# Encoder layer: two small constants widened, adaLN dots, token-block loads and one row of sums moved

## The chip, the cores and the metric

The kernel runs on one core of one Trainium2 chip. The metric is the device time of one execution in microseconds (us). The core has a matrix engine (TensorE, PE in the profile, with its weight loads as PEld), a vector engine (VectorE, DVE), a scalar engine (ScalarE, ACT), GpSimd (POOL) and SyncE (SP), which issues most of the loads from its queue. All tiles live in on-chip memory of 128 partitions; a tile's address is its offset within each partition.

## The reference

One residual layer of a bidirectional encoder, for one sequence of 1024 tokens and 1024 channels. What matters:

```python
mod = silu(c) @ w_ada + b_ada                       # 6 x 1024, shifts, scales, gates
h = rmsnorm(x, norm1_g) * (1 + sc1) + sh1
u, v, q, k, va, gate_a, gate_b = split(h @ w_in)
a_out = gelu(u) * (W_s rmsnorm(gelu(v)) + b) @ w_a  # per chunk of 128 positions
b_out = window_attention(q, k, va) @ w_b            # |t - s| <= 128, ALiBi, sinks
merged = sigmoid(gate_a) * a_out + sigmoid(gate_b) * b_out
x = x + gt1 * (merged @ w_o)
h2 = rmsnorm(x, norm2_g) * (1 + sc2) + sh2
x = x + gt2 * ((silu(h2 @ w_gate) * (h2 @ w_up)) @ w_out)
```

All values are fp32.

## The kernel before

Every product is made of three fp32r matmuls: each operand is split into a high part (a cast on ACT, tiles named ...h) and a low part (a subtraction on DVE, ...l), and high x high, high x low and low x high are added up in PSUM. A weight arrives as a `raw` tile of 128 x 1024, is split into `wh` and `wl` (`unit`), and serves 12 to 24 matmuls of 512 columns. `raw`, `wh` and `wl` have three buffers each.

The stages, in order:

- `half(0)` and `half(1)` work through 512 tokens each: norm and adaLN, the q, k, v and u projections, attention and the gating branch, then the loop over `d` (line 1117 on) with the branch products `w_a`, `w_b`: 24 matmuls per d. The unit of d + 1 is split in iteration d. Beside it run jobs. In half 0 these prepare half 1's tokens (`x_mod`), and adaLN dots run. In half 1 they are `block_sums`: the gates of d = 2 to 7 are computed for both halves of tokens and channels at once from sums of blocks, seven products in place of eight, and the jobs make those sums.
- `block_sums(k, part, ...)` needs four tiles of 128 x 512: a0 and a1 (half 0's tokens, `x0d`, in the two buffers of `hs`), b0 and b1 (half 1's, `x1sd`, in the two of `xs`). `block_load(k)` fetches all four; `block_part` makes the high part at once and gives back the step that makes the low part. Part 0 of chunk k runs in iteration 2k, part 1 in 2k + 1.
- the gates for d = 2 to 7 (loop in line 1185).
- the output projection `w_o` of half 0 and then of half 1 (loop in line 1261), a unit and 24 matmuls per d. The operand `m0` of half 0 is in `mid` tiles, `m1` of half 1 in `j` tiles. Each iteration adds the squares of its rows to `ss` (`sumsq`). Half 0's row of root mean squares is made in half 1's loop: `col_rstd` (four small matmuls with `ss`, in two passes each, then a power on POOL) after the matmuls of d = 0, `spread` after those of d = 1, and from then on `mod2(d - 1)` makes the second adaLN input of half 0.
- the FFN's products for both halves, again by seven block products per block of weights (operands `h`, `j` and `mid`), and the output product.

adaLN: each of the 48 columns of `mod` is a dot of silu(c) with a row of weights, on DVE (1.22 us for 128 x 1024). Sixteen are made at the start. The other 32 come in the order of `ada_queue`, each from one `raw` tile: `ada_load` fetches the next, `ada_next` makes a dot and fetches the next one (unless told not to), `ada_half` does one in two halves of 512 with tiles of `hs` and a small tile `part`. They lie in half 0's branch loop (one per d for d = 0 to 6 and a second at d = 2: eight), in half 1's projections (five), in the gates' loop (five and five halves), and in half 0's output projection (one per d and a second at d = 4: nine).

Order: `load` keeps the loads on SP's queue in program order, so a load that waits for its buffer holds those behind it. Instructions of an engine keep the written order where `in_order` is set (the first projection, the attention's part of the code and d < 2 of the branch loop, the last two d of the output projection); elsewhere the order is laid out when the program is built.

Addresses: the pools follow each other: `const` (ends with `shd`), `wpool` (raw, wh, wl), `hpool` (h), `mid`, `t2` (t2, hs, xs), `small` (ss, part and others), `cpool` (silu_c), then either the attention's tiles or the tiles `j`, and in the last stage raw2, oh and ol. Every tile takes a multiple of 32 bytes. `raw`, `wh` and `wl` are 4096 bytes a buffer, `h`, `mid` and `j` 8192. In the program of before `wpool` begins at 32 past a multiple of 64, and with it all the large tiles.

Of the kernel before, what the change touches and what calls it, by code (L numbers as in the profile page):

```python
# [8 lines left out]
F32 = mybir.dt.float32  # L9
# [3 lines left out]
ALU = mybir.AluOpType  # L13
# [3 lines left out]
P = 128  # L17
# [21 lines left out]
def kernel(  # L39
# [47 lines left out]
    const = ctx.enter_context(pool("const"))  # L87
# [25 lines left out]
    def stream(tag):  # L113
        return t2.tile([P, 512], F32, tag=tag, name=nm(tag), bufs=2)
# [18 lines left out]
    def sm(n, name):  # L133
        return small.tile([P, n], F32, tag=name, name=nm(name))

    def load(dst, src):
        tc.keep_in_program_order(nc.sync.dma_start(dst, src))
# [395 lines left out]
    def ada_half(more=True):  # L533
        if not ada_halves:
            return
        col, gain, t = ada_halves.pop(0)
        part = sm(1, "part")
        for i, acc_col in enumerate((acc_mod[:, col : col + 1], part)):
            V.scalar_tensor_tensor(out=t[i], in0=t[i], scalar=1.0,
                                   in1=silu_c[:, i * 512 : (i + 1) * 512], op0=ALU.mult,  # L540
                                   op1=ALU.mult, accum_out=acc_col)
        added(acc_mod[:, col : col + 1], part)
        ada_end(col, gain)
        if more:
            ada_half_load()
# [7 lines left out]
    def added(dst, src):  # L553
        V.tensor_tensor(dst, dst, src, op=ALU.add)
# [14 lines left out]
        V.tensor_tensor(s, m[:, :, 0], m[:, :, 1], op=ALU.add)  # L569
        rstd(s, NT, rcol[1])  # L570

    shd = const.tile([P, 8], F32, tag="shd", name="shd")
    dsh, nsh = shd[:, :4], shd[:, 4:]
    blk = {}

    def block_load(k):
        chunk = [stream(x) for x in ("hs", "hs", "xs", "xs")]
        for i, src in enumerate((x0d, x1sd)):
            for q in range(2):
                load(chunk[2 * i + q], src[4 * q + k])  # L580
        return chunk

    def block_part(name, k, src, kind, bias=None):
        if k == 0:
# [6 lines left out]
        return lambda: V.scalar_tensor_tensor(out=l, in0=src, scalar=bias, in1=h.bitcast(F32),  # L591
                                              op0=ALU.add, op1=ALU.subtract)

    def block_sums(k, part, chunk, kinds):
        a0, a1, b0, b1 = chunk
        c = slice(k, k + 1)
        if part == 0:
            if k == 0:
                V.tensor_tensor(dsh, mod[:, SH1 + 4 : SH1 + 8], mod[:, SH1 : SH1 + 4], op=ALU.subtract)
                V.tensor_scalar(nsh, mod[:, SH1 + 4 : SH1 + 8], -1.0, None, op0=ALU.mult)  # L600
            low = block_part("B21", k, a1, kinds[0], mod[:, SH1 + 4 + k : SH1 + 5 + k])
            V.tensor_tensor(b1, b1, b0, op=ALU.subtract)
            low()
            low = block_part("T3", k, b1, kinds[1], dsh[:, c])
            V.tensor_tensor(a1, a0, a1, op=ALU.subtract)
            V.tensor_tensor(b0, a0, b0, op=ALU.subtract)
            low()
            return
        low = block_part("B11", k, a0, kinds[0], mod[:, SH1 + k : SH1 + k + 1])
        added(a1, b1)  # L610
        low1 = block_part("T1", k, b0, kinds[1])
        low()
        low = block_part("T4", k, a1, kinds[2])
        low1()
        V.scalar_tensor_tensor(out=a0, in0=b1, scalar=-1.0, in1=a0, op0=ALU.mult, op1=ALU.subtract)
        low()
        block_part("N2", k, a0, kinds[1], nsh[:, c])()

    raws, gunits, acc = {}, {}, {}

# [69 lines left out]
    def half(hf):  # L690
# [62 lines left out]
        for k in range(KT):  # L753
            if hf == 0:
                x = xt[k]
# [340 lines left out]
        if hf == 0:  # L1096
            ada_load()
            x_spread()
            x_load(0)
            x_load(1)  # L1100
            jobs.extend((k, lambda k=k: x_mod(k)) for k in range(KT))
            jobs.append((7, lambda: x_mod(KT)))
        else:
            apool_ctx.close()
            jpools.append(ffn_ctx.enter_context(pool("j", 6, reuse_waits="tile")))
            kinds = (lambda: midt(F32R, 4)), (lambda: jt(F32R, 4)), hid
            blk["B22"] = (hH[1], hL[1])
            chunk = [block_load(0)]

            def block_job(k, part):  # L1110
                block_sums(k, part, chunk[0], kinds)
                if part and k < 3:
                    chunk[0] = block_load(k + 1)

            jobs.extend((2 * k + p, lambda k=k, p=p: block_job(k, p)) for k in range(4) for p in range(2))

        for d in range(KT):
            in_order[0] = d < 2
            if 0 < d < KT - 1:
                wab.append(unit(None, V, abr.pop(0)))  # L1120
                if d + 2 + hf < KT:
                    abr.append(raw_unit(w_ab[d + 2 + hf]))
            elif d:
                if hf == 0:
                    early.append(unit(None, V, early_raw[0]))
                else:
                    gate_prep_b(2)
            if hf and d == 5:
                gate_load(2)
            if hf and d == 6:  # L1130
                gate_prep_a(2)
            ms = []
            for br, t in ((1, (oH, oL)), (0, (gH, gL))):
                pb = mm_bank()
                for k in range(4):
                    kc = slice(br * Q + k * P, br * Q + (k + 1) * P)
                    mm3(pb, (wab[d][0][:, kc], wab[d][1][:, kc]), (t[0][:, k, :], t[1][:, k, :]),
                        k == 0, k == 3)
                if d < 2:
                    sg = gates.pop(0)  # L1140
                    V.scalar_tensor_tensor(out=sg, in0=sg, scalar=1.0, in1=pb, op0=ALU.add,
                                           op1=ALU.mult)
                    ms.append(sg)
                else:
                    c = tmp()
                    A.copy(c, pb)
                    j = 2 * hf + br
                    store(pd[d][:, j * Q : (j + 1) * Q], c)
            if d < 2:
                V.tensor_tensor(ms[0], ms[0], ms[1], op=ALU.add)  # L1150
                store(md[hf][d], ms[0])
            in_order[0] = False
            while jobs and jobs[0][0] <= d:
                jobs.pop(0)[1]()
            if hf == 0:
                if d == 2:
                    ada_next()
                ada_next(d < 6)
                if d > 5:
                    early_raw.append(raw_unit((w_q[0], w_kv[0])[d - 6]))  # L1160

# [84 lines left out]
    for hf in range(2):  # L1246
# [14 lines left out]
        for d in range(KT):  # L1261
            wo = wo_next
            if d < KT - 1:
                wo_next = unit(w_o[d + 1])
            elif hf == 0:
                wo_next = unit(w_o[0])
            else:
                raw1 = raw_unit(w_gate[1])
                raw2.append(raw_unit(w_gate[2]))
            if hf == 1 and d == 6:  # L1270
                early.append(unit(w_gate[0], V))
            in_order[0] = hf == 1 and d > 5
            if hf == 1 and d in (2, 4):
                early.append(first_unit(d // 2 - 1))
            xk = stream("xs")
            load(xk, x_rows(hf, d))
            pw = mm_bank()
            for k in range(KT):
                kc = slice(k * P, (k + 1) * P)
                mm3(pw, (wo[0][:, kc], wo[1][:, kc]),  # L1280
                    (m[k // 4][0][:, k % 4, :], m[k // 4][1][:, k % 4, :]), k == 0, k == KT - 1)
            if hf == 1:
                if d == 0:
                    col_rstd(sums[0], NT, rcol[2])
                elif d == 1:
                    rb = spread(rcol[2], NT)
                if d:
                    mod2(d - 1)
            x1 = tmp() if hf == 0 else x1B[d // 4][:, d % 4, :]
            V.scalar_tensor_tensor(out=x1, in0=pw, scalar=mod[:, GT1 + d : GT1 + d + 1], in1=xk,  # L1290
                                   op0=ALU.mult, op1=ALU.add)
            sumsq(x1, d == 0, ss)
            store(x1d[d * P : (d + 1) * P, hf * HALF : (hf + 1) * HALF], x1)
            if hf == 0:
                if d == 0:
                    m1 = m_tiles(jt)
                else:
                    m_split(m1, d - 1)
                m_load(m1, 1, d)
                if d == KT - 1:  # L1300
                    m_split(m1, d)
                ada_next()
                if d == 4:
                    ada_next()
            if hf == 1 and d == KT - 1:
                mod2(d)
                early.append(unit(None, V, raw1))
# [195 lines left out]
    def low(src, t, k):  # L1503
        V.tensor_tensor(t[1][:, k, :], src, t[0][:, k, :].bitcast(F32), op=ALU.subtract)
# [360 lines left out]
```

## Time and profile before

| what | us |
|---|---|
| median of 3 runs (1273.71 to 1276.75) | 1275.17 |
| the profiled execution | 1270.48 |
| its span, first to last instruction | 1268.7 |
| PE busy in the span | 1234.8 |
| DVE busy | 911.9 |
| ACT busy | 572.5 |
| POOL busy | 161.1 |

The mean granted clock of TensorE is 0.994. A row of the profile reads: engine, operation, out<-in by the program's names with shapes, count, then busy time and mean ns of one, then the engine's idle time before it with what ended it. In a timeline the first number is the start in us from the span's start, the second the duration of the (merged) row. Nearly all instructions have one line, 76, since a helper there records them; tiles tell them apart. Matmuls overlap: one lasts about 390 ns, and the next begins before it has ended, so the time that a matmul takes is read from one start to the next.

### The profile page before, as it was taken

What the parts mean: (1) busy time and instruction counts of PE and PEld (TensorE: products, weight loads), DVE (VectorE), ACT (ScalarE), POOL (GpSimd) and SP (SyncE); (2) the same over time, 40 slices, a digit from 0 to 9 for tenths busy, and PEclk for the clock granted to TensorE, in tenths of its full rate; (3) what the DMA queues carried; (4) which work ended last, traced back from release to release, by engine and by line L of the source; (5) the groups of instructions that cost most, each with busy time, mean ns of one, the idle gap of its engine ahead of it and who ended that gap; (6) DMA issues with size and microseconds to landing.
All of it is one profiled execution on the core that took longest, in us unless ns stands there. A gap on an engine that the chain in (4) does not pass through costs nothing.

```text
span 1268.7 us, 15580 instructions
## 1 busy us (share of the span) xinstructions
PE 1234.8 (97%) x5634; PEld 1014.8 (80%) x5634; DVE 911.9 (72%) x1496; ACT 572.5 (45%) x930; POOL 161.1 (13%) x202
## 2 busy tenths in 40 slices
PE   6999998999999999999999999999999999999998
PEld 4888886888887787787888887888888887888887
DVE  9898885487888787976698756666666676455646
ACT  5567954267866333434444333333333334433341
POOL 1124332023321000001100000000110000010001
PEclk9999999999999999999999999999999999999999
DMA  9632179522247536697612353454654549896652
GB/s 369 240 100 96 38 245 320 166 85 66 59 146 244 215 138 228 216 331 233 242 57 100 135 197 136 162 199 182 215 167 176 188 166 332 287 325 189 195 164 100
DMA packets 76271, 236.28 MB, mean 186 GB/s; under 512 B 9121, under 2 KB 9121, under 8 KB 70178
## 3 DMA queue, kind: packets, MB, share of 16 engines
q1 hardware_dynamic: 60626, 163.45, 38.4%
q0 software_dynamic: 15568, 71.84, 15.3%
q8 instruction: 44, 0.72, 0.2%
q14 instruction: 33, 0.27, 0.1%
HBM read 178.11 MB, written 57.15 MB: 185 GB/s over the span
## 4 chain that ended last, share of the span: by engine, by line
PE 60%; issue 13%; DMA 11%; DVE 10%; ACT 5%; POOL 1%; SPq 0%; DVEq 0%; ACTq 0%; POOLq 0%
PE at L76 31%; PE mm L76 28%; DVE mid L76 3%; DVE wl L76 2%; DMA raw<-in_w_ada_dram 2%; DMA raw<-in_w_o_dram 2%; DMA raw<-in_w_ab_dram 2%; ACT wh L76 1%; ACT lb L76 1%; ACT mid L76 1%; DVE raw L76 1%; DMA mid<-in_w_ada_dram 1%; DVE xs L76 1%; DMA wo<-in_w_out_dram 1%; DMA hs<-md 1%
## 5 line engine op out<-in xcount | busy, mean ns | idle before, releaser
L76 ACT CAST wh<-raw 128x1024 fp32r<-128x1024 f32 x155 | 162.3, 1050 | 199.4 <-PE mm L76 52.7
L76 DVE TENSOR_TENSOR wl<-raw,wh 128x1024 fp32r<-128x1024 f32 x141 | 172.0, 1221 | 89.2 <-ACT wh L76 85.6
L76 PE MATMUL mm<-mid,wh 128*128 128x512 f32 x704 | 219.3, 393 | 2.6 <-ACT t L76 1.2
L76 PEld LDWEIGHTS mm<-mid,wh 128*128 128x128 f32 x704 | 132.4, 189 | 32.7 <-ACT t L76 1.6
L76 PE MATMUL at<-j,wh 128*128 128x512 f32 x464 | 145.5, 394 | 0.0
L76 PE MATMUL mm<-mid,wl 128*128 128x512 f32 x352 | 138.4, 393 | 3.2 <-DVE wl L76 3.2
L76 PE MATMUL mm<-wh,h 128*128 128x512 f32 x384 | 131.1, 404 | 2.9 <-ACT h L76 2.1
L76 PEld LDWEIGHTS at<-j,wh 128*128 128x128 f32 x464 | 87.1, 188 | 20.5
L76 DVE TENSOR_TENSOR wl<-ws,wh 128x1024 fp32r<-128x1024 f32 (+1 forms) x55 | 62.0, 1127 | 44.5 <-ACT wh L76 44.5
L76 PE MATMUL at<-j,wl 128*128 128x512 f32 x232 | 91.8, 395 | 0.5 <-DVE wl L76 0.5
L76 PE MATMUL mm<-j,wh 128*128 128x512 f32 x288 | 91.6, 399 | 0.0
L76 PE MATMUL at<-h,wh 128*128 128x512 f32 x288 | 89.1, 390 | 0.7 <-DVE mid L76 0.7
L76 PEld LDWEIGHTS mm<-wh,h 128*128 128x128 f32 x384 | 72.8, 192 | 17.9 <-ACT h L76 3.0
L76 PE MATMUL mm<-h,wh 128*128 128x512 f32 x272 | 84.6, 392 | 0.0
L76 PEld LDWEIGHTS mm<-mid,wl 128*128 128x128 f32 x352 | 66.5, 189 | 19.0 <-DVE wl L76 5.0
L76 ACT CAST wh<-ws 128x1024 fp32r<-128x1024 f32 (+1 forms) x55 | 53.5, 973 | 57.9 <-DVE ws L76 41.3
L76 PE MATMUL mm<-wl,h 128*128 128x512 f32 x192 | 76.4, 398 | 0.0
L76 PEld LDWEIGHTS mm<-j,wh 128*128 128x128 f32 x288 | 54.7, 190 | 12.6
L76 PEld LDWEIGHTS at<-h,wh 128*128 128x128 f32 x288 | 53.8, 188 | 12.2 <-DVE mid L76 1.1
L76 DVE TENSOR_TENSOR ol<-raw,oh 128x1024 fp32r<-128x1024 f32 x30 | 36.7, 1224 | 32.4 <-ACT oh L76 32.1
L76 PEld LDWEIGHTS mm<-h,wh 128*128 128x128 f32 x272 | 50.6, 188 | 10.5
L76 ACT ACTIVATE xs<-xs 128x512 f32<-128x512 f32 x21 | 13.3, 633 | 99.2 <-DVE xs L76 99.2
(273 smaller groups left out, 2544.9 us busy)
## 6 DMA issues: line engine op xcount, KB each, us to landing
raw<-in_w_gate_dram SPq DMA_DIRECT2D x28, 512.0 KB, 5.2
raw<-in_w_ada_dram SPq DMA_DIRECT2D x27, 512.0 KB, 5.5
tA<-hid POOLq DMA_DIRECT2D x11, 1024.0 KB, 5.2
tB<-hid POOLq DMA_DIRECT2D x11, 1024.0 KB, 5.1
wo<-in_w_out_dram POOLq DMA_DIRECT2D x22, 512.0 KB, 6.1
wS<-wo POOLq DMA_DIRECT2D x11, 1024.0 KB, 5.2
raw<-wS SPq DMA_DIRECT2D x44, 256.0 KB, 3.7
raw<-tB SPq DMA_DIRECT2D x44, 256.0 KB, 4.5
```

The costliest lines, as they stand in the source:

```text
L76: ins = f(*args, **kw)
```

## The change

Five edits. `shd` gets 16 columns, of which 8 are used, and `part` 16, of which 1 is used. `block_load` fetches one tile by name, and each of a chunk's four tiles is fetched as soon as its predecessor has been read for the last time; `block_sums` does B21, T3, B11 and T4 in part 0, and T1 and N2 in part 1. In half 0's branch loop the second dot of d = 2 and the dot of d = 6 are gone, and in half 0's output projection d = 3 and d = 5 have two dots as d = 4 does. Half 0's `col_rstd` stands after the matmuls of d = 1, its `spread` after those of d = 2, and `mod2` follows with 0 at d = 2, 1 and 2 at d = 3, then one per d.

```diff
@@ ada_half
-        part = sm(1, "part")
+        part = sm(16, "part")[:, :1]
@@ half 1's blocks
-    shd = const.tile([P, 8], F32, tag="shd", name="shd")
-    dsh, nsh = shd[:, :4], shd[:, 4:]
+    shd = const.tile([P, 16], F32, tag="shd", name="shd")
+    dsh, nsh = shd[:, :4], shd[:, 4:8]
     blk = {}
 
-    def block_load(k):
-        chunk = [stream(x) for x in ("hs", "hs", "xs", "xs")]
-        for i, src in enumerate((x0d, x1sd)):
-            for q in range(2):
-                load(chunk[2 * i + q], src[4 * q + k])
-        return chunk
+    chunk = {}
+
+    def block_load(k, name):
+        if k < 4:
+            chunk[name] = stream("hs" if name[0] == "a" else "xs")
+            load(chunk[name], (x0d if name[0] == "a" else x1sd)[4 * int(name[1]) + k])
...
-    def block_sums(k, part, chunk, kinds):
-        a0, a1, b0, b1 = chunk
+    def block_sums(k, part, kinds):
         c = slice(k, k + 1)
+        a0, a1, b0, b1 = (chunk[x] for x in ("a0", "a1", "b0", "b1"))
...
             V.tensor_tensor(b1, b1, b0, op=ALU.subtract)
             low()
             low = block_part("T3", k, b1, kinds[1], dsh[:, c])
+            low1 = block_part("B11", k, a0, kinds[0], mod[:, SH1 + k : SH1 + k + 1])
             V.tensor_tensor(a1, a0, a1, op=ALU.subtract)
-            V.tensor_tensor(b0, a0, b0, op=ALU.subtract)
+            added(a1, b1)
             low()
+            low = block_part("T4", k, a1, kinds[2])
+            low1()
+            low()
+            block_load(k + 1, "a1")
             return
-        low = block_part("B11", k, a0, kinds[0], mod[:, SH1 + k : SH1 + k + 1])
-        added(a1, b1)
+        V.tensor_tensor(b0, a0, b0, op=ALU.subtract)
         low1 = block_part("T1", k, b0, kinds[1])
+        V.scalar_tensor_tensor(out=a0, in0=b1, scalar=-1.0, in1=a0, op0=ALU.mult, op1=ALU.subtract)
+        low = block_part("N2", k, a0, kinds[1], nsh[:, c])
+        low1()
+        block_load(k + 1, "b0")
         low()
-        low = block_part("T4", k, a1, kinds[2])
-        low1()
-        V.scalar_tensor_tensor(out=a0, in0=b1, scalar=-1.0, in1=a0, op0=ALU.mult, op1=ALU.subtract)
-        low()
-        block_part("N2", k, a0, kinds[1], nsh[:, c])()
+        block_load(k + 1, "b1")
+        block_load(k + 1, "a0")
@@ half(1), before the loop over d
-            chunk = [block_load(0)]
-
-            def block_job(k, part):
-                block_sums(k, part, chunk[0], kinds)
-                if part and k < 3:
-                    chunk[0] = block_load(k + 1)
-
-            jobs.extend((2 * k + p, lambda k=k, p=p: block_job(k, p)) for k in range(4) for p in range(2))
+            for x in ("a1", "b0", "b1", "a0"):
+                block_load(0, x)
+            jobs.extend((2 * k + p, lambda k=k, p=p: block_sums(k, p, kinds))
+                        for k in range(4) for p in range(2))
@@ half(0), in the loop over d
             if hf == 0:
-                if d == 2:
-                    ada_next()
-                ada_next(d < 6)
+                ada_next(d < 5)
@@ the output projection
             if hf == 1:
-                if d == 0:
+                if d == 1:
                     col_rstd(sums[0], NT, rcol[2])
-                elif d == 1:
+                elif d == 2:
                     rb = spread(rcol[2], NT)
-                if d:
-                    mod2(d - 1)
+                for i in {2: (0,), 3: (1, 2), 4: (3,), 5: (4,), 6: (5,), 7: (6,)}.get(d, ()):
+                    mod2(i)
...
                 ada_next()
-                if d == 4:
+                if 2 < d < 6:
                     ada_next()
```

## The prediction

> **What bounds the kernel now.** I read the page first: the span and the engines' shares.
>
> ```profile
> span 1268.7 us, 15580 instructions
> PE 1234.8 (97%) x5634; PEld 1014.8 (80%) x5634; DVE 911.9 (72%) x1496; ACT 572.5 (45%) x930; POOL 161.1 (13%) x202
> ```
>
> TensorE (PE) is busy for 97% of the span, so there are only two ways to gain: the 33.9 us in which it is idle (1268.7 - 1234.8), and the time of one matmul. I therefore read the busy time by stages next: us of the stretch, then each engine's busy time and count, the granted clock, the DMA engines' share and GB/s.
>
> ```profile
> 214.00:226.00 12.00, 8.03 (x28) 6.21 (x27) 5.09 (x8) 1.69 (x3) 1.54 (x3) 0.73 0.70 239
> 342.00:409.00 67.00, 64.64 (x297) 53.52 (x295) 55.26 (x84) 43.89 (x71) 16.11 (x19) 0.97 0.58 190
> 527.00:576.00 49.00, 48.71 (x215) 39.87 (x214) 39.04 (x62) 18.31 (x25) 4.86 (x9) 1.00 0.91 321
> 576.00:586.00 10.00, 6.85 (x28) 5.29 (x27) 4.96 (x6) 4.09 (x5) 1.57 (x2) 0.83 0.94 311
> 632.00:1000.00 368.00, 367.64 (x1599) 299.37 (x1598) 259.16 (x363) 131.48 (x187) 24.55 (x46) 1.00 0.46 162
> 1060.00:1140.00 80.00, 80.00 (x354) 66.18 (x354) 41.23 (x38) 34.62 (x35) 4.41 (x7) 1.00 0.92 327
> 342.00:1268.00 926.00, 912.15 (x3987) 743.85 (x3985) 641.04 (x869) 364.48 (x484) 71.41 (x118) 1.00 0.57 195
> ```
>
> Apart from the start, PE is short of work at three places, and at each of them the clock falls below 1.00: the seam of the two halves (214 to 226), the branch products of half 1 (342 to 409), and the seam of the two output projections (576 to 586). From 632 on PE is full, and only the time of one matmul counts.
>
> **Part 1: adaLN dots.** At the seam of the halves the timeline (start, duration, engine, instruction, in brackets idle time and what ended it) shows this:
>
> ```profile
> 211.45 7.97 SPq L137 DMA_DIRECT2D raw<-in_w_ada_dram  x2
> 216.57 0.40 PE L76 MATMUL mm<-wl,h 128*128 128x512 f32 x1
> 217.83 1.22 DVE L76 SCALAR_TENSOR_TENSOR raw<-raw,silu_c 128x1024 f32<-128x1024 f32 x1 [6.41 <-DMA raw<-in_w_ada_dram]
> 218.99 1.22 DVE L76 TENSOR_TENSOR wl<-raw,wh 128x1024 fp32r<-128x1024 f32 x1
> 220.26 0.58 PE L76 MATMUL at<-wl,h 128*128 128x256 f32 x1 [3.29 <-DVE wl L76]
> 223.20 0.84 PE L76 MATMUL at<-wh,h 128*128 128x256 f32 x3
> 223.84 0.63 PE L76 MATMUL mm<-wh,h 128*128 128x512 f32 x1
> 224.27 0.63 PE L76 MATMUL mm<-wl,h 128*128 128x512 f32 x1
> ```
>
> DVE stands 6.41 us at the dot of d = 6, whose weights landed late. Behind it in DVE's queue is the low part of w_kv, and PE waits for that: from 216.57 + 0.23 to 220.26, 3.46 us. Afterwards PE runs at half clock: 223.84 to 224.27 is 0.43 for a matmul that takes 0.227 elsewhere (part 4). Some ten such matmuls until 226 lose 0.2 each, the seven 256 wide ones (223.20 to 223.84 for three, 0.21 each, against about 0.12) another 0.65: 2.6 us. The change takes the second dot of d = 2 and that of d = 6 out of this loop. DVE then has nothing before the low part of w_kv, which can run near 213. That is 3.46 + 2.6 = 6.1, and I take **-6.0**. Late next would be the second unit of w_q, which DVE can split a microsecond later. Bounds: -7.5 if the 0.7 us before 216.23 go too, -2 if another load of the three `raw` buffers is late in its place.
>
> The two dots go to the output projection of half 0, where d = 3, 4 and 5 now have two each. Two dots are 2 x (1.22 + 0.3) = 3 us of DVE, which has 49 - 39 = 10 us free there. Their weights are the dearer part:
>
> ```profile
> 528.20:558.20 30.00, 30.00 (x135) 24.82 (x133) 24.64 (x42) 11.11 (x16) 3.24 (x6) 1.00 0.97 336
> 554.67 1.23 DVE L76 SCALAR_TENSOR_TENSOR raw<-raw,silu_c 128x1024 f32<-128x1024 f32 x1
> 558.95 1.23 DVE L76 TENSOR_TENSOR wl<-raw,wh 128x1024 fp32r<-128x1024 f32 x1 [2.14 <-ACT wh L76]
> 560.23 0.50 PE L76 MATMUL mm<-mid,wl 128*128 128x512 f32 x1 [0.29 <-DVE wl L76]
> ```
>
> The DMA engines are 97% busy here, and 2 x 0.52 MB at 336 GB/s are 3.1 us more. Today's one double dot (554.67) already made the next w_o unit late: its low part waited 2.14 us and PE about 0.45. The SP queue hands out `w_o`, `x`, `md` and these loads in order, so each load of w_o stands behind two of w_ada. I take **+1.5** for three doubles in place of one; bounds 0 (prefetched in time) and +5 (all the added transfer time and more ends on PE).
>
> **Part 2: token blocks by need.** In half 1's branch products:
>
> ```profile
> 391.19 0.72 ACT L76 ACTIVATE mid<-hs,mod 128x512 fp32r<-128x512 f32 x1 [2.61 <-DMA hs<-x0d]
> 391.95 0.75 DVE L76 SCALAR_TENSOR_TENSOR mid<-hs,mod,mid 128x512 fp32r<-128x512 f32 x1 [3.06 <-ACT mid L76]
> 397.96 1.22 DVE L76 TENSOR_TENSOR wl<-raw,wh 128x1024 fp32r<-128x1024 f32 x1
> 398.07 2.12 SPq L137 DMA_DIRECT2D hs<-x0d  x2
> 399.23 0.50 PE L76 MATMUL mm<-mid,wl 128*128 128x512 f32 x1 [2.36 <-DVE wl L76]
> ```
>
> DVE loses 3.06 us to a block that SP could ask for only when the buffer freed last was free (all four loads are issued together, and they hold the queue for 2.12 us, with w_ab, w_ga and w_gb behind them). The low part at 397.96 comes that much later, and PE waits 2.36 for it; the clock of 0.97 over 67 us is another 1.5 or so at half speed. Loaded one by one, a1 is asked for some five operations of DVE earlier. Work is only moved: part 0 has seven operations on DVE instead of five, part 1 four instead of six, about 0.7 each. 3.06 us less on DVE cover the 2.36. But what part 0 gains in length (1.4 us) can again stand ahead of a low part of w_ab, so of the 4 us I take **-3**; bounds -4.5 and +2 (the longer part 0 makes two units late by 1 us).
>
> **Part 3: sum of squares of half 0, one block later.**
>
> ```profile
> 576.76 1.04 ACT L76 CAST wh<-raw 128x1024 fp32r<-128x1024 f32 x1 [3.66 <-DMA raw<-in_w_o_dram]
> 577.84 1.22 DVE L76 TENSOR_TENSOR wl<-raw,wh 128x1024 fp32r<-128x1024 f32 x1 [2.82 <-ACT wh L76]
> 579.72 1.05 PE L76 MATMUL at<-ones,ss 128*128 128x1 f32 x8 [3.15 <-DVE ss L76]
> 580.63 0.71 PE L76 MATMUL mm<-j,wh 128*128 128x512 f32 x2
> 581.18 0.39 PE L76 MATMUL mm<-j,wl 128*128 128x512 f32 x1
> ```
>
> PE waits 3.15 us for `ss`. Moving that wait away doesn't free PE: the weights of the next block are themselves late, their high part at 577.80 and their low part at 579.06. So the third matmul of the block comes at about 579.1 in place of 581.18, 2.1 us earlier, and the eight small matmuls (0.9) are paid later: 1.2 net. The remaining waits are shorter (1.4 and 0.8), so the half clock that follows today (0.83 over 10 us, some 1.5) is likely spared: **-2.7**. Bounds: 0, if the load of w_o comes later still, behind two more of w_ada; -5, the whole loss, if it comes earlier. mod2 of d = 0 to 6 is packed tighter, hidden by a DVE that is free for a third of that stage.
>
> **Part 4: the addresses.** shd grows from 32 to 64 bytes per partition, and part, in four buffers, from 128 to 256. From the order of the pools, everything from wpool to the small tiles moves by 32 bytes, and what lies behind the small tiles (silu_c, j) by 160. Relative to wh, the tiles mid, h and wl lie at multiples of 512 bytes before and after; j lies at 288 x 512 + 384 before, and at 289 x 512 after. The timeline has j beside others:
>
> ```profile
> 421.28 2.96 PE L76 MATMUL at<-j,t 128*128 128x512 f32 x12
> 424.07 0.63 PE L76 MATMUL mm<-mid,wh 128*128 128x512 f32 x2
> 424.54 0.39 PE L76 MATMUL mm<-mid,wl 128*128 128x512 f32 x1
> 425.22 0.39 PE L76 MATMUL mm<-mid,wl 128*128 128x512 f32 x1
> ```
>
> The groups of the whole span (count, busy us, mean ns), and the stretch from 632 on with the tile j alone:
>
> ```profile
> L76 PE MATMUL at<-j,wh 128*128 128x512 f32 x464 | 145.5, 394 | 0.0
> L76 PE MATMUL mm<-j,wh 128*128 128x512 f32 x288 | 91.6, 399 | 0.0
> L76 PE MATMUL at<-h,wh 128*128 128x512 f32 x288 | 89.1, 390 | 0.7 <-DVE mid L76 0.7
> ```
>
> ```profile
> 632.00:1000.00 368.00, 176.62 (x732) 1.00 0.46 162
> ```
>
> Twelve with j take 2.79 us (421.28 to 424.07), 232.5 ns each; three with mid 0.68 (424.54 to 425.22), 227. The means by group say the same, 394 and 399 against 390. In 632 to 1000, 368.00 us for 1599 matmuls are 230 each; in 1060 to 1140, without j, 226. Nearly half of that stretch is j's (732), which leaves (368.00 - 867 x 0.227) / 732 = 0.234 for one with j, waits included. The two groups with j and wh hold 752; a product of three matmuls has two with wh and one with wl, so they are 1128 with wl, and some 120 more have j beside t or h. If the place relative to the weights is the reason, all become like mid: 1250 x 5.2 ns (4 to 9 by the means, 5.5 by the timeline), **-6.5**. Bounds 0 and -8; in the likeliest case the 227 of the others stays.
>
> The sum is -6.0 + 1.5 - 3 - 2.7 - 6.5 = -16.7. The profiled execution took 1270.5 (its span and 1.8 around it), the median is 1275.2, 4.7 more; so 1270.5 - 16.7 + 4.7 = **1258.5**, with 1250 to 1267 as its own range.
>
> **Rivals.**
>
> A: *alignment to 64 bytes shortens every matmul.* All large tiles begin at 32 past a multiple of 64 today, so no row shows an aligned one. But at half clock a matmul takes 0.43 and 0.42 (from 223.84 on), just twice 213 ns, while at full clock it takes 227: 14 ns belong to no work of the array, they vanish when it runs slowly, and they depend on addresses (j). If half of that goes, 3987 x 7 = 28 us after 342 alone, 1231; if all of it, 56 us, 1203. Against it: DVE and DMA are not far behind in some stages, and nothing shows that 32 bytes matter.
>
> By the Trainium skill, page "TensorE: Matmul & The Clock Gate", section "Wait — 56ns, not 53.3ns?", back-to-back matmuls of 512 columns start 426.7 ns apart on the slow clock and 215.7 on the full one; the trace agrees with the first and has 227 for the second, and by that rule 11 ns are to be had on each, an estimate of 54 us for some 4900 matmuls of that width. The page "SBUF — State Buffer", section "Specifications (TRN2)", speaks against the change: lines are of 16 bytes, of which 32 is already a multiple; by that the fill gives nothing but j's share.
>
> B: *the addresses do nothing*, j included: the fill doesn't do what it says. Then only parts 1 to 3 are left, 1275.2 - 10.2 = 1265.
>
> C: *slower: the new places cost what j's cost.* If every matmul of 512 columns pays some 5.8 ns more, about what separates j from mid, 3987 of them lose 23 us after 342, and the 900 or so of that width among the 1647 before (5634 - 3987) lose 5; with the 10.2 won elsewhere, 1293. It decides from 2.1 ns per matmul on (10.2 us over 4900). Against it: the pairs other than j keep their distance.
>
> D: *the double dots starve the projection.* Three w_o units, each late by one load of 0.52 MB at 336 GB/s (1.55 us) and with as much half clock behind it as at 579 (some 1.5), cost 9.2 in place of 1.5: 1266.
>
> **How the numbers follow.** Likeliest 0.45; A 0.32; B 0.12; C 0.05; D 0.06. A measurement here tells about 0.2%, 2.5 us, from no change. The range is 1212 to 1268: it leaves out C, the far end of A, and the upper parts of B and D, about 0.2. Faster by over 0.2% (below 1272.6): all of the likeliest and of A, nearly all of B and D, 0.91; within 0.2% 0.04; slower 0.05.
>
> **What would show it.** Part 1: no wait of PE for a low part near 217, clock 1.00 there. Part 2: no idle DVE before a block from x0d. Part 3: no 3 us wait for ss, a shorter one for w_o's unit in its place. The added dots: more PE waits for w_o units between 527 and 576. Part 4: the groups with j at 390 to 393 ns; for A, all groups shorter, for C, all longer. I am wrong if 632 to 1000, where only addresses change, moves by other than some 4 us (732 of j's matmuls lie there), or if the three waits persist.

## The result and the profile after

The changed kernel takes 1265.3 us in the median of 6 runs (1262.1 to 1267.4), the kernel before beside it 1274.4 (1268.8 to 1276.8): a ratio of 0.9932, with a 95% interval of 0.9906 to 0.9957. That is 8.7 us faster, where 16.7 were forecast. The profiled execution of the changed kernel took 1266.8 us. First its page, with the span and the shares of the engines:

```profile
span 1265.0 us, 15583 instructions
PE 1227.7 (97%) x5634; PEld 1012.8 (80%) x5634; DVE 911.8 (72%) x1496; ACT 574.0 (45%) x930; POOL 161.5 (13%) x202
```

Then the same stretches as in the prediction, with 226 to 242 added (us of the stretch, busy time and count of PE, PEld, DVE, ACT, POOL, granted clock, DMA share, GB/s):

```profile
214.00:226.00 12.00, 10.33 (x55) 8.41 (x55) 5.04 (x8) 1.05 (x1) 0.54 (x1) 1.00 0.62 197
226.00:242.00 16.00, 11.05 (x53) 9.43 (x52) 7.76 (x12) 2.11 (x2) 0.00 (x0) 0.89 0.45 136
342.00:409.00 67.00, 62.55 (x293) 51.43 (x292) 55.47 (x84) 44.06 (x70) 15.99 (x19) 0.99 0.56 191
527.00:576.00 49.00, 44.53 (x185) 34.05 (x186) 39.05 (x66) 17.39 (x26) 4.34 (x8) 1.00 0.94 326
576.00:586.00 10.00, 10.00 (x46) 8.27 (x45) 7.06 (x9) 4.27 (x5) 1.08 (x2) 1.00 0.89 314
632.00:1000.00 368.00, 367.62 (x1622) 303.06 (x1621) 261.58 (x365) 134.18 (x189) 25.66 (x48) 1.00 0.46 166
```

Two of the three places where PE was idle are filled: 214 to 226 now has 55 matmuls in place of 28, and 576 to 586 has 46 in place of 28. But 226 to 242, which the prediction didn't look at, has PE busy for 11.05 of its 16 us (15.79 in the kernel before), and 527 to 576 has 185 matmuls in place of 215. In 632 to 1000 there are 23 matmuls more at the same length.

PE runs 5634 matmuls in nearly the same order in every kernel here, so a stage can be measured in each of them from the start of one numbered matmul to that of another. The table gives us per stage, taken from one profiled execution of each kernel; the experiments' kernels are described below.

| matmuls | stage | before | changed | fills | dots | blocks | ss | dots+ss | changed, in order | before, in order | combined |
|---|---|---|---|---|---|---|---|---|---|---|---|
| 960-1200 | seam of the halves | 56.2 | 55.8 | 56.0 | 55.9 | 58.7 | 54.3 | 55.2 | 47.2 | 49.0 | 47.2 |
| 1900-2100 | last branch products, first gates | 51.7 | 53.6 | 50.6 | 52.4 | 54.1 | 51.5 | 51.3 | 52.8 | 51.3 | 50.1 |
| 2475-2649 | output projection, half 0 | 40.2 | 46.1 | 40.3 | 45.8 | 40.5 | 41.4 | 45.9 | 45.8 | 40.2 | 41.1 |
| 2649-2670 | seam of the two projections | 8.9 | 4.8 | 8.6 | 3.9 | 8.2 | 4.9 | 4.9 | 4.8 | 10.5 | 4.8 |
| 2670-4479 | projection of half 1, FFN | 414.6 | 408.3 | 409.4 | 414.2 | 414.4 | 414.2 | 413.8 | 408.3 | 414.2 | 410.7 |
| 4479-5630 | output of the FFN | 264.2 | 263.2 | 263.2 | 264.2 | 264.2 | 264.2 | 264.2 | 263.2 | 264.2 | 263.3 |

Read against the prediction: the addresses gave 6.3 + 1.0, the seam of the projections 4.1; half 0's output projection cost 5.9 and the first gates 1.9; the seam of the halves gave next to nothing. Together the rows make 4.0 us, and the two profiled executions are only 3.6 apart (1270.5 and 1266.8), where the runs give 8.7: about half of the gain isn't in these two profiles. The seam of the halves is the least steady row: over the seven profiled kernels in which nothing touches it, it lies between 54.3 and 59.2, mean 57.2.

**The seam of the halves.** The timeline of the changed kernel (start, duration, engine, instruction, in brackets idle time and what ended it):

```profile
206.82 8.64 SPq L137 DMA_DIRECT2D raw<-in_w_ada_dram  x2
...
213.87 1.22 DVE L76 SCALAR_TENSOR_TENSOR raw<-raw,silu_c 128x1024 f32<-128x1024 f32 x1 [7.08 <-DMA raw<-in_w_ada_dram]
215.02 1.22 DVE L76 TENSOR_TENSOR wl<-raw,wh 128x1024 fp32r<-128x1024 f32 x1
216.30 0.38 PE L76 MATMUL at<-wl,h 128*128 128x256 f32 x1 [1.55 <-DVE wl L76]
...
229.31 7.71 SPq L137 DMA_DIRECT2D raw<-in_w_ada_dram  x2
235.43 1.23 DVE L76 SCALAR_TENSOR_TENSOR raw<-raw,silu_c 128x1024 f32<-128x1024 f32 x1 [6.15 <-DMA raw<-in_w_ada_dram]
236.83 2.35 DVE L76 TENSOR_TENSOR wl<-raw,wh 128x1024 fp32r<-128x1024 f32 x2
238.11 0.58 PE L76 MATMUL at<-wl,h 128*128 128x256 f32 x1 [4.95 <-DVE wl L76]
```

The dot of d = 6 is gone, and yet a dot stands ahead of w_kv's low part at 213.87: half 1's own first one, which the order laid out at building has put there. It stood there in the kernel before as well; the prediction took it for the dot of d = 6 (point 2 of the account below). What the removal did is to let its weights be asked for earlier, at 206.82 in place of 211.45, and PE's wait at 217 shrinks from 3.29 to 1.55 us. At half 1's fourth dot the same figure stands again: a dot that waits 6.15 us for weights that could only be asked for at 229.31, two low parts behind it, and PE idle for 4.95. The kernel before has this dot and this low part too, at 237.08 and 238.49, but PE, which was later, hardly waited for them:

```profile
239.76 0.39 PE L76 MATMUL at<-wl,h 128*128 128x256 f32 x1 [0.21 <-DVE wl L76]
```

So PE came earlier to a low part that came only 1.7 us earlier, and most of what it had won was lost there.

**The first gate steps.** Changed kernel first, then the matching rows of the kernel before:

```profile
394.85 0.32 SPq L137 DMA_DIRECT2D hs<-x0d  x1
395.22 0.43 SPq L137 DMA_DIRECT2D raw<-in_w_ga_dram  x1
...
404.53 1.04 ACT L76 CAST wh<-raw 128x1024 fp32r<-128x1024 f32 x1 [2.66 <-DVE raw L76]
406.11 0.71 ACT L76 ACTIVATE mid<-hs,mod 128x512 fp32r<-128x512 f32 x1
406.86 0.49 PE L76 MATMUL mm<-mid,wh 128*128 128x512 f32 x1 [2.27 <-ACT mid L76]
408.02 0.74 DVE L76 SCALAR_TENSOR_TENSOR mid<-hs,mod,mid 128x512 fp32r<-128x512 f32 x1
408.82 0.80 PE L76 MATMUL mm<-mid,wh 128*128 128x512 f32 x1 [1.46 <-DVE mid L76]
```

```profile
387.96 0.39 SPq L137 DMA_DIRECT2D raw<-in_w_ga_dram  x1
...
403.95 0.73 ACT L76 ACTIVATE mid<-hs,mod 128x512 fp32r<-128x512 f32 x1 [1.30 <-DMA hs<-x0d]
404.71 0.75 DVE L76 SCALAR_TENSOR_TENSOR mid<-hs,mod,mid 128x512 fp32r<-128x512 f32 x1 [0.43 <-ACT mid L76]
```

The 3.06 us wait of DVE for a block at 391 is gone, as forecast. But a load of the next a1 now stands in SP's queue ahead of w_ga and w_gb, and waits there until its buffer is free: the gate weights, first w_ga and then w_gb, are asked for from 395.22 in place of 387.96. Their splitting lands on ACT and DVE in front of the last token block, whose high part comes at 406.11 in place of 403.95 and whose low part at 408.02 in place of 404.71. The first gate step multiplies that block, so PE waits 2.27 and 1.46 us.

**The double dots.** In half 0's output projection, the waits of PE from 558 on:

```profile
558.29 0.73 PE L76 MATMUL mm<-mid,wh 128*128 128x512 f32 x2 [1.05 <-ACT wh L76]
559.55 0.50 PE L76 MATMUL mm<-mid,wl 128*128 128x512 f32 x1 [0.53 <-DVE wl L76]
565.92 0.50 PE L76 MATMUL mm<-mid,wl 128*128 128x512 f32 x1 [0.53 <-DVE wl L76]
572.34 0.73 PE L76 MATMUL mm<-mid,wh 128*128 128x512 f32 x2 [1.10 <-ACT wh L76]
573.60 0.50 PE L76 MATMUL mm<-mid,wl 128*128 128x512 f32 x1 [0.53 <-DVE wl L76]
```

w_o's units come late one after the other, by a half to one microsecond each time, high part and low part. Their loads show why. Changed kernel first, then the kernel before at a d with one dot:

```profile
558.27 1.23 DVE L76 TENSOR_TENSOR wl<-raw,wh 128x1024 fp32r<-128x1024 f32 x1 [1.86 <-ACT wh L76]
559.52 0.33 SPq L137 DMA_DIRECT2D raw<-in_w_o_dram  x1
...
564.64 1.23 DVE L76 TENSOR_TENSOR wl<-raw,wh 128x1024 fp32r<-128x1024 f32 x1
565.89 0.33 SPq L137 DMA_DIRECT2D raw<-in_w_o_dram  x1
```

```profile
561.30 1.22 DVE L76 SCALAR_TENSOR_TENSOR raw<-raw,silu_c 128x1024 f32<-128x1024 f32 x1
562.55 0.33 SPq L137 DMA_DIRECT2D raw<-in_w_o_dram  x1
```

Beside one dot, a load of w_o is issued when a dot has freed its `raw` buffer. Beside two, the three `raw` buffers turn once per d, and the load is issued only when the unit of w_o before it has been split (558.27 + 1.23, then 559.52; 564.64 + 1.23, then 565.89; likewise 551.92). Load, cast and split of one unit then stand in a row behind those of the last, 7.6 and 6.4 us from one of these three loads to the next, where 24 matmuls take 5.4. The DMA engines move less meanwhile, not more: 299 GB/s in 550 to 560, against 348 in the kernel before. No run with a fourth `raw` buffer tests this reading.

### The profile page after: what moved, and what is told of

It reads as the page before. It is cut to its first block, busy times and chain, and to the rows that moved or that the text cites. A ratio compares the mean times of both kernels' runs of the same rounds, so it can differ in the third digit from the quotient of the medians.

```text
span 1265.0 us, 15583 instructions
## 1 busy us (share of the span) xinstructions
PE 1227.7 (97%) x5634; PEld 1012.8 (80%) x5634; DVE 911.8 (72%) x1496; ACT 574.0 (45%) x930; POOL 161.5 (13%) x202
## 4 chain that ended last, share of the span: by engine, by line
PE 63%; issue 12%; DMA 10%; DVE 9%; ACT 4%; POOL 0%; SPq 0%; ACTq 0%; DVEq 0%; POOLq 0%
PE mm L76 32%; PE at L76 31%; DVE mid L76 3%; DVE wl L76 2%; DMA raw<-in_w_gb_dram 2%; DMA raw<-in_w_o_dram 2%; DMA raw<-in_w_ada_dram 2%; ACT wh L76 1%; ACT mid L76 1%; DMA raw<-in_w_ab_dram 1%; DVE raw L76 1%; DMA mid<-in_w_ada_dram 1%; DMA wo<-in_w_out_dram 1%; ACT lb L76 1%; DMA wS<-wo 1%
## 5 line engine op out<-in xcount | busy, mean ns | idle before, releaser
L76 PE MATMUL at<-j,wh 128*128 128x512 f32 x464 | 142.8, 389 | 0.0
L76 ACT CAST wh<-ws 128x1024 fp32r<-128x1024 f32 (+1 forms) x55 | 53.6, 974 | 59.0 <-DVE ws L76 42.5
L76 PEld LDWEIGHTS mm<-j,wh 128*128 128x128 f32 x288 | 55.1, 192 | 11.6
L76 PEld LDWEIGHTS mm<-h,wh 128*128 128x128 f32 x272 | 50.6, 188 | 10.3
```

What stands on the lines that cost most here:

```text
L76: ins = f(*args, **kw)
```

## The experiments

Times are medians, each set beside runs of the kernel before on the same chip; gains are worked out from the ratio and the kernel before's median of that set (1273.7, 1271.9, 1272.4 and 1273.1 us), with their 95% intervals.

**One part of the change at a time.**

Fills alone:

```diff
-        part = sm(1, "part")
+        part = sm(16, "part")[:, :1]
-    shd = const.tile([P, 8], F32, tag="shd", name="shd")
+    shd = const.tile([P, 16], F32, tag="shd", name="shd")
```

> The kernel before with the two filled-up constants alone (all large tiles at 0 past a multiple of 64, j at 289 x 512 from wh). Theory 'place relative to the weights': only matmuls with j as moving operand change, 232.5 to 227 ns each, so the groups at<-j,wh and mm<-j,wh go from 394 and 399 to about 389 and 396 ns, the other groups stay within 1 ns, and the time falls by 6.5 to 7.5 us (some 1267 to 1268). Rival 'alignment': groups without j get shorter too and the time falls by 28 us or more. Rival 'addresses do nothing': within 1 us. None of the three waits at the seams goes.

Measured 1268.0, ratio 0.9958 (0.9940 to 0.9976): 5.4 us faster (3.1 to 7.6). j's groups fell to 389 and 394 ns, those with h and wh stayed at 390 and 392.

Dots alone (the two dots out of the branch loop, `ada_next(d < 5)`, and `if 2 < d < 6` in place of `if d == 4`):

> The kernel before with the moved adaLN dots alone. Theory after the traces: the seam of the halves gains nothing net, since the wait for a low part behind a dot moves from 217-220 to about 233-238 (6.4 won, 6.0 lost again), and the three double dots in half 0's output projection cost 5 to 6 us there in small waits for w_o units: 4 to 6 us slower than before (1279 to 1281). Rival, the prediction's terms: -6.0 + 1.5, so 4.5 faster (1270). A third reading, that both the gain and the loss are artefacts of one profiled execution, would give within 1.5 us.

Measured 1268.0, ratio 0.9961 (0.9946 to 0.9977): 5.0 us faster (2.9 to 6.9). By the total the prediction's terms came out right and the theory after the traces wrong; the stages say something else. In the table this kernel loses 5.6 us in half 0's output projection, as expected, gains nothing to speak of in the seam of the halves, and gets back 5.0 at the seam of the projections, where its sum of squares isn't moved at all: PE comes late to that place, and ss is there. Its profiled execution took 1271.6 us, 3.6 above its median, so part of the gain of the others isn't in the profile, and where they have it stays open.

Token blocks alone:

> The kernel before with the token blocks loaded by need alone. Theory after the traces: the waits at 391 and 399 go (3.3 won), but w_ga and w_gb of d = 2 are asked for later in SP's queue and the first gate steps wait for their low parts and run at half clock (6.4 lost), 1.2 won afterwards: 1 to 3 us slower than before. Rival, the prediction's term: 3 us faster.

Measured 1275.4, ratio 1.0017 (0.9999 to 1.0035): 2.2 us slower (0.1 faster to 4.5 slower). The table has 54.1 in place of 51.7 us for the stage, with the same two waits for the last block as in the changed kernel.

Sum of squares alone:

> The kernel before with half 0's sum of squares read one block later, alone. Theory after the traces: PE's 3.15 us wait at 576 goes and nothing takes its place, since w_o's second unit was ready early enough once the queue of ACT and DVE isn't held up by ss: 3.5 to 4.5 us faster. Rival, the prediction's term: 2.7 faster, because the late weights of the second block take over part of the wait (a PE wait of 1 to 2 us for w_o's low part near 578).

Measured 1268.0, ratio 0.9964 (0.9946 to 0.9982): 4.6 us faster (2.3 to 6.9). No wait for weights takes the place of the one for ss.

**Which address counts.** `part` alone, then `shd` alone, then `part` at 128 bytes (`sm(32, "part")`):

> The kernel before with only `part` filled up: j lies at 289 x 512 from wh as in the changed kernel, but all large tiles still begin at 32 past a multiple of 64. Theory 'place relative to the weights': the whole gain of both fills, 4 to 7 us faster than before, j's groups at 389 and 396 ns. Rival 'alignment to 64 bytes': no gain (within 1.5 us), j's groups at 394 and 399.

> The kernel before with only `shd` filled up: all large tiles begin at multiples of 64, but j still lies at 288 x 512 + 384 from wh. Theory 'place relative to the weights': no gain (within 1.5 us), j's groups at 394 and 399 ns. Rival 'alignment to 64 bytes': the whole gain of both fills, 4 to 7 us.

> The kernel before with `part` made 128 bytes wide, nothing else: j then lies at 289 x 512 + 256 from wh, and all large tiles still begin at 32 past a multiple of 64. Theory 'only whole multiples of 512 are free': j's groups stay at 394 and 399 ns or get dearer, and the time is within 2 us of before. Rival 'the period is 256 or less': j's groups at 389 and 396 ns and 4 to 7 us faster than before, as with the distance of 289 x 512.

Measured: `part` alone 1268.5, ratio 0.9965 (0.9944 to 0.9987), 4.5 us faster; `shd` alone 1273.6, ratio 1.0011 (0.9993 to 1.0030), no gain; the distance of 289 x 512 + 256 took 1268.7, ratio 0.9960 (0.9942 to 0.9977), 5.1 us faster. The groups of the kernel with `shd` alone, and then of the one with the distance of 256 (count, busy us, mean ns):

```profile
L76 PE MATMUL at<-j,wh 128*128 128x512 f32 x464 | 145.5, 394 | 0.0
L76 PE MATMUL mm<-j,wh 128*128 128x512 f32 x288 | 92.6, 403 | 0.0
```

```profile
L76 PE MATMUL at<-j,wh 128*128 128x512 f32 x464 | 143.0, 389 | 0.0
L76 PE MATMUL mm<-j,wh 128*128 128x512 f32 x288 | 89.6, 392 | 0.0
L76 PE MATMUL at<-h,wh 128*128 128x512 f32 x288 | 89.4, 391 | 1.2 <-DVE mid L76 0.9
```

With every large tile at a multiple of 64 and j at 384 past a multiple of 512, j is as dear as before; with tiles at 32 past a multiple of 64 and j at a multiple of 256, it is as cheap as h. The stage from matmul 2670 to 4479 says the same: 409.7 us with `part` alone, 414.8 with `shd` alone, 410.0 with the distance of 256, and 414.6 before. So the distance counts and the alignment doesn't, and a multiple of 256 is enough: the theory of whole multiples of 512 was wrong.

**Do the dots and the sum of squares add up?** Both together, nothing else:

> The kernel before with the moved adaLN dots and the later sum of squares, nothing else. Alone they gave 5.0 and 4.6 us. Theory 'the same wait': with the moved dots PE runs late in half 0's output projection, so ss is ready when it is asked for and the 3.15 us wait at 576 is gone already; the two together give 5 to 7 us only (1267 to 1269). Rival 'additive': 9 to 10 us (1264).

Measured 1270.6, ratio 0.9992 (0.9977 to 1.0007): 1.0 us faster (2.9 faster to 0.9 slower), where the terms on record make 7.2. The stages of its profiled execution, which is typical of it (1270.4), show why: 5.7 us lost in half 0's output projection, 4.0 won at the seam behind it, 1.0 at the seam of the halves. The moved dots use up what the sum of squares can give. That the two together came out slower than either alone is more than "the same wait" explains, and stays open with the profile of the dots alone.

**Whose order is it?** The changed kernel, with half 1's projections kept in program order, on every engine:

```diff
         if hf == 0:
+            in_order[0] = True
             early.append(unit(None, V, early_raw[1]))
```

> The changed kernel, with the instructions of half 1's projections kept in the order of the program, so that DVE forms the low parts of w_kv and w_q ahead of the dots that wait for w_ada. Theory 'DVE's order': the 5 us wait of PE near 233 (low part behind a late dot) goes, 4 to 6 us faster than the changed kernel (0.988 to 0.990 of before). Rival 'the loads': the three raw buffers free up no earlier, the units' own loads are late instead, and the time stays within 1.5 us of the changed kernel (0.992 to 0.994 of before).

Measured 1257.2 (1255.5 to 1258.2), ratio 0.9883 (0.9861 to 0.9906): 14.9 us faster than before, 6.2 more than the change itself. Its stretches and its DVE:

```profile
214.00:226.00 12.00, 11.96 (x65) 10.26 (x65) 4.88 (x8) 1.21 (x2) 0.54 (x1) 1.00 0.54 174
226.00:242.00 16.00, 16.00 (x91) 13.97 (x90) 7.86 (x12) 3.05 (x3) 0.00 (x0) 1.00 0.65 206
```

```profile
213.71 1.23 DVE L76 TENSOR_TENSOR wl<-raw,wh 128x1024 fp32r<-128x1024 f32 x1 [4.22 <-ACT wh L76]
214.85 1.22 DVE L76 SCALAR_TENSOR_TENSOR raw<-raw,silu_c 128x1024 f32<-128x1024 f32 x1
...
229.16 2.36 DVE L76 TENSOR_TENSOR wl<-raw,wh 128x1024 fp32r<-128x1024 f32 x2 [5.02 <-ACT wh L76]
231.44 1.22 DVE L76 SCALAR_TENSOR_TENSOR raw<-raw,silu_c 128x1024 f32<-128x1024 f32 x1
```

Each low part now stands ahead of the dot, DVE waits for ACT's high part and not for w_ada, and PE is full in both stretches. The same edit in the kernel before:

> The kernel before, with the instructions of half 1's projections kept in the order of the program and nothing else. Theory 'DVE's order alone': the low part of w_kv no longer stands behind a dot, so the waits at 204 and 216 go without moving any dot, 5 to 7 us faster than before (0.9945 to 0.996). Rival 'too many loads': with eight dots in half 0's branch loop their loads make the units themselves late, so the order alone brings less than 3 us, and the moved dots are needed for the rest.

Measured 1265.8, ratio 0.9945 (0.9927 to 0.9963): 7.0 us faster with no dot moved. The seam takes 49.0 us there and 47.2 with the dots moved as well. So the order was the larger cause of the wait at 217, the number of dots the smaller. The wait near 204 that the expectation names was for a tile `t` of ACT and not for a low part; such waits of PE make 1.9 us around the seam in the kernel before and 1.5 here.

**Without the token blocks** (the changed kernel with the loads as before):

> The changed kernel with the token blocks loaded as before. Theory: the loads by need cost the changed kernel 1 to 3.5 us (gate units of d = 2 asked for late), so this is faster than it: 0.9905 to 0.9925 of before (the changed kernel had 0.9932). Rival, the prediction's term of 3 us won by them: 0.994 to 0.996.

Measured 1265.1, ratio 0.9938 (0.9915 to 0.9960), against 0.9932 of the changed kernel: the intervals cover each other, and this comparison decides nothing. The stage is shorter without them, 51.5 against 53.6 us.

**What the findings make together.** Both fills, the later sum of squares, program order at the seam, the token blocks as before, and the two dots in half 1's output projection:

```diff
+            if hf == 1 and d in (1, 3):
+                ada_next()
             if hf == 1 and d == KT - 1:
                 mod2(d)
```

> The kernel before with both constants filled up, the later sum of squares, half 1's projections in program order and six dots in half 0's branch loop; the two dots taken from there go to half 1's output projection (d = 1 and 3), and the token blocks are loaded as before. Theory: addresses 5.5, ss 4.5 (the double dots that would eat it are gone), seam of the halves 8 to 9: 18 to 19 us faster than before, 0.985 to 0.9865, and 2 to 5 us faster than the changed kernel in program order (0.9883). Rival: the loads for the two dots make w_o's or w_gate's units late in half 1's output projection just as they do in half 0's, and it is no faster than 0.988.

Measured 1254.5 in 4 runs (1251.9 to 1256.8), ratio 0.9859 (0.9835 to 0.9883): 17.9 us faster than before. It has the lowest median of all, but its interval meets that of the changed kernel in program order (0.9861 to 0.9906). Its profile:

```profile
span 1250.0 us, 15580 instructions
PE 1221.3 (98%) x5634; PEld 1009.5 (81%) x5634; DVE 910.6 (73%) x1496; ACT 572.5 (46%) x930; POOL 161.5 (13%) x202
```

Half 0's output projection is back at 41.1 us. The dots aren't free in their new place either: the stage from half 1's projection on takes 410.7 in place of 408.3, 2.4 us.

## Why the prediction was right and where it was wrong

The direction, the range and the account of the addresses were right; the gain was put at nearly twice its size. Of its five terms one came out at its size, one gain was put too large, one gain and one cost too small, and one had the wrong sign. So it is partly luck that the time still lies inside the likeliest case's 1250 to 1267. Term by term:

1. **Addresses, forecast -6.5: right, and for the reason given.** The table has 6.3 us between matmuls 2670 and 4479 and 1.0 after them; the fills alone gave 5.4 (3.1 to 7.6). The sign it had named holds too: the matmuls that fill 632 to 1000 in the kernel before take 363.3 in place of 367.8 us, 4.5 less where some 4 were asked for. The groups after the change:

```profile
L76 PE MATMUL at<-j,wh 128*128 128x512 f32 x464 | 142.8, 389 | 0.0
L76 PE MATMUL mm<-j,wh 128*128 128x512 f32 x288 | 90.6, 396 | 0.0
L76 PE MATMUL at<-h,wh 128*128 128x512 f32 x288 | 89.1, 391 | 0.7 <-DVE mid L76 0.7
```

at<-j fell from 394 to 389, mm<-j from 399 to 396, h stayed. That refutes rival B (the addresses do nothing), A (all matmuls gain) and C (all lose). A had a chance of 0.32, on the strength of one number, 213 ns as half the time at half clock; no distance met with in the runs has a median below 226 ns for 512 columns.

2. **Seam of the halves, forecast -6.0: the step that failed is the reading that DVE stands "at the dot of d = 6", and with it "DVE then has nothing before the low part of w_kv".** The rows of the kernel before show which dot it is. A small row behind each dot finishes its column of `mod`: for the eight gate columns, which come first in `ada_queue` and are half 0's eight dots, it is a TENSOR_SCALAR, for the scales that follow a SCALAR_TENSOR_TENSOR with `badap`:

```profile
207.12 1.23 DVE L76 SCALAR_TENSOR_TENSOR raw<-raw,silu_c 128x1024 f32<-128x1024 f32 x1 [0.56 <-DMA raw<-in_w_ada_dram]
208.94 0.20 DVE L76 TENSOR_SCALAR mod<-acc_mod,cc 128x1 f32<-128x1 f32 x1
...
220.12 0.21 DVE L76 SCALAR_TENSOR_TENSOR mod<-acc_mod,badap,cc 128x1 f32<-128x1 f32 x1
```

The dot of d = 6 ran at 207.12 and kept nobody waiting at 217. The one at 217.83, finished at 220.12, is the ninth, half 1's own first. In the program it stands behind the split of w_kv; but where `in_order` isn't set, the order is laid out when the program is built, and there it came ahead, in both kernels. Removing two other dots could not take it away; keeping the order does. What the removal gave: 57.2 us is the mean of the stage in the seven profiled kernels without it, 55.1 in the four with it (55.8, 55.9, 55.2, 53.6), so some 2 us, the lower bound on record, whose reason ("another load of the three `raw` buffers is late in its place") fits the later wait. With program order as well, 10.0 of the 57.2 go.

3. **The two dots in half 0's output projection, forecast +1.5: mis-sized.** Over the eight profiled kernels without the added dots the projection takes 40.5 us, over the five with them 45.6: +5.1, just past the upper bound of +5. That w_o's units come late behind the double dots was named in the term and in rival D, and the one double dot of the kernel before already showed it; the choice near the low end was wrong. Term and rival priced the transfer (3.1 us for two loads, or 1.55 a unit). What the rows show in its place is the wait for a `raw` buffer, which sets load, cast and split of each unit behind those of the last, while the DMA engines move less than before. The half clock that D added did not follow: 1.00 in 527 to 576.

4. **Sum of squares, forecast -2.7: mis-sized, by a misread row.** The reading "the weights of the next block are themselves late" took the low part of 577.84 for that of the block that ss holds up. Units are prepared one block ahead; that block's low part is the one before it in the same timeline of the kernel before:

```profile
573.13 1.23 DVE L76 TENSOR_TENSOR wl<-raw,wh 128x1024 fp32r<-128x1024 f32 x1 [0.25 <-ACT wh L76]
...
578.98 0.68 DVE L76 TENSOR_TENSOR ss<-ss,t 128x512 f32<-128x512 f32 x1
```

It was ready at 574.36. Only ss was late, because its last addition stood on DVE behind the low part of 577.84, which waited for its own load. The whole loss goes: 4.6 alone. It isn't added to the dots' account, though: after the dots' 5 us of delay ss is in time anyway.

5. **Token blocks, forecast -3: wrong sign.** The wait it named went (DVE's 3.06 us, and PE's 2.36 at 399 is 0.72 at 397 now); the step that failed is leaving out who stands behind a waiting load in SP's queue. The term noted that w_ab, w_ga and w_gb stood behind the four loads, but not that one load by need still waits for its buffer, now ahead of w_ga and w_gb. Alone the edit cost 2.2 (-0.1 to +4.5), about the upper bound of +2, for which another reason was given.

6. **The sum.** The terms were added as if independent. The dots with the sum of squares gave 1.0 in place of 7.2, the largest piece of the 8.0 us that are missing, and the token blocks 2.2 the other way in place of 3. The pieces measured on their own (1.0 + 5.4 - 2.2 = 4.2) make less than the 8.7 of the whole (5.5 to 12.0); each carries some 2 us either way, so whether the parts also help each other stays open. The measured 1265.3 is the number of rivals B and D (1265 and 1266); B's reason is refuted, D's (a starved projection) happened at about half of D's price, 5.1 against 9.2, so that both numbers fit is luck.

## What to carry to other kernels

A wait for a split weight is ended by whatever stands ahead of the split on its engine: ask who orders that engine, and make sure which instruction it is before removing one, and look for the next wait that may take its place. A load that waits for a buffer holds up every load behind it in its queue, so a load made earlier or finer must be checked against the loads that it now precedes. Savings on one chain are not added up before asking whether the first delay hides the second wait.

## What the hardware showed unexpectedly

The time from one 512-column matmul to the next depends on the distance between the address of its moving tile (the operand that is streamed through the array) and that of the weights loaded for the following matmul. Worked out from the traces of six kernels, with the addresses that the program gives the tiles: at a distance of 0 or 256 past a multiple of 512, 227 ns in the median (3591 matmuls at 0 in the kernel before, 1276 at 256 in the kernel made for it); at 384 and 128, 232 (1215 and 63 in the kernel before). So the pattern seems to repeat after 256 bytes. That the following matmul's weights count, and not its own, shows in the kernel before in 32 matmuls that lie at 0 from their own weights and at 128 or 384 from the next: 232 too. At 64, 192, 320 and 448 there are at most 24 matmuls of a kernel, with medians between 226 and 232, and no rule can be read from them. Alignment to 64 bytes by itself showed no gain: `shd` alone, 1.0011 (0.9993 to 1.0030).

By the Trainium skill, page "SBUF — State Buffer", section "Specifications (TRN2)", lines are of 16 bytes, so that the fill to 64 gives nothing; the run with `shd` alone agrees. By the Trainium skill, page "TensorE: Matmul & The Clock Gate", section "Wait — 56ns, not 53.3ns?", back-to-back matmuls of 512 columns start 215.7 ns apart at full clock; here none of these distances has a median below 226, and the measurement decides.

The spread of the executions differs from kernel to kernel: the kernel before lay between 1267 and 1279 us in all its runs, the changed one in program order between 1255.5 and 1258.2 in six, the combined one, with the same order, between 1251.9 and 1256.8 in four. What sets it is not shown.
